# A hybrid layer step on one core: top-16 selection and norms cut into pieces and queued between weight splits, the output projection interleaved with the first query

## The chip, the cores and the metric

The kernel runs on one core of one Trainium2 chip. The metric is the device time of one execution in microseconds (us), the median of three runs. TensorE (PE) has two clock levels here, 1.2 and 2.4 GHz; the profile gives the granted clock as a share of the higher one.

## The reference, cut to what matters

One layer for two request groups that share all weights: 128 prompt tokens (one tile of 128) and 512 sample tokens (four tiles). After a mixer of a convolution and a recurrence, the layer projects with `w_out`, normalises, and runs a layer of product-key retrieved experts (PEER):

```python
y = jnp.concatenate([z, y_r], axis=-1) @ w_out
x = _layer_norm(ALPHA * x + g1 * y, ln1_g, ln1_b)
u = _layer_norm(x) * (1.0 + sc2) + sh2
...
q = (xb @ w_query).reshape(TOKEN_BLOCK, PEER_HEADS, 2, D_KEY)
s = jnp.einsum('chpd,hpnd->chpn', q, sub_keys).astype(jnp.float32)
sv, si = lax.top_k(s, PEER_TOPK)
cand = (sv[:, :, 0, :, None] + sv[:, :, 1, None, :]).reshape(TOKEN_BLOCK, PEER_HEADS, PEER_TOPK * PEER_TOPK)
top_s, top_pos = lax.top_k(cand, PEER_TOPK)
g = jax.nn.softmax(top_s, axis=-1).astype(xb.dtype)
act = jax.nn.gelu(jnp.einsum('chkd,cd->chk', jnp.take(peer_u, ids, axis=0), xb))
out = jnp.einsum('chk,chkd->cd', g * act, jnp.take(peer_v, ids, axis=0))
```

D is 2048, there are 8 heads with 2 x 128 sub-keys, 16384 experts, and 16 experts per head and token.

## The kernel before, in words

Every fp32 product is made of three fp32r products of high and low parts (`mm3`, L87 to L90), so each weight tile of 128x1024 is loaded by the SP queue (`load_w`, L80), split by ScalarE (ACT) into `whi` (L76) and by VectorE (DVE) into `wlo` (L77), and then used by 24 or 18 matmuls. There are three buffers for raw tiles and three for split ones. The tile framework writes each engine's instruction list ahead of time from the order of the program and a list scheduler; on the chip each engine goes through its list in order.

Tokens come in three parts. Tiles 0 and 1 are group B (`TB`, 256 columns), tiles 2 to 4 group A (`TA`, 384 columns). Of tile 1, 64 tokens are handled with the prompt tile by gathering their 128 expert rows from memory with indirect DMAs on the POOL queue (192 pairs of gathers of 1 MiB, `gather_gen`, L760; three row buffers, so DVE uses each in turn, L796 and L807). The other 448 tokens go through all experts densely: 256 weight halves for the scores (`s_half`, L865, called "S halves" here), 14 blocks of building the sparse gate matrix (L905 to L950, the G stage), and 256 steps with `peer_v` (the V stage, L1010 on).

The order of the stretch that the change touches, from the end of group B's output projection: `norm_pair` for tiles 0 and 1 (L698); `w_out` for group A, column groups 0 and 1 of four (L707, each column group has eight weight tiles of 18 matmuls); `query` for group B, heads 0 to 2 (L708); `w_out` column groups 2 and 3 (L709); `norm_a` for tiles 2 to 4 (L713); `query` for group B, heads 3 to 7 (L716); `query` for group A, all heads (L897), with eight S halves put in (`FILL`); then the G stage with the remaining S halves.

`query` (L602) takes, for each head and key half, two weight tiles, 48 matmuls into one bank, a copy to `qT`, a product with the sub-keys (L632), a copy to `s` (L634) and one `top16` per token tile, written right there; after both key halves it adds the candidates (L639), takes `top16` again, and finds indices and gates with one-hot products (L674, L676, L681). All of this is DVE work in the order of the program. `pace(rate)` (L852) advances the gathers by `rate` per weight half (0.5 in group A's query, 0.8 at S halves); what is left of them when the V stage begins is spread over its first 236 steps (`r_v`, L1008).

Of the kernel before, what the change touches and what calls it, by code (L numbers as in the profile page):

```python
# [34 lines left out]
def layer_kernel(ctx: ExitStack, tc: tile.TileContext, i: dict, y_p: bass.AP, y_s: bass.AP, st_o: bass.AP):  # L35
# [80 lines left out]
    def mm_bank():  # L116
        return ps_mm.tile([128, 512], F32, name="mm", tag="mm")
# [393 lines left out]
    def w_out(yh, yl, ts, ngs, rate=0.0):  # L511
        for ng in ngs:
# [6 lines left out]
            for kq in range(8):  # L519
                wh, wl = pre.pop(0) if pre else split(load_wo(kq, cs))  # L520
                for kk in range(2):
                    k = 2 * kq + kk
                    for n in range(len(ts)):
                        sl = slice(n * 128, (n + 1) * 128)
                        mk = mm3(banks[n], yh[:, k, sl], yl[:, k, sl], wh[:, kk, :], wl[:, kk, :], k == 0, k == KT - 1)
                if rate:
                    marks.append(mk)
                    pace(rate)
# [41 lines left out]

    def norm_a(hi, lo):
        sc, sh = modT[4], modT[3]
        for n, t in enumerate(TA):
            xx = x1[t]
            norm(cp, xx)
            for h in range(2):
                cs = slice(h * 1024, (h + 1) * 1024)
                V.tensor_tensor(xx[:, cs], xx[:, cs], ln1[0][:, cs], op=ALU.mult)
                V.tensor_tensor(xx[:, cs], xx[:, cs], ln1[1][:, cs], op=ALU.add)
            Q.dma_start(x1_d[t * 128:(t + 1) * 128, :], xx)  # L580
            norm(cp, xx)
            for q in range(4):
# [9 lines left out]
                V.tensor_tensor(lo[dst], u, hi[dst].bitcast(F32), op=ALU.subtract)  # L592

    def top16(vals, idx, src, n):
# [7 lines left out]
    def query(uh, ul, ts, heads, rate=0.0, fill=None):  # L602
        nt = len(ts)
        N = nt * 128
        o = OFF if ts[0] else 0
# [4 lines left out]
        for h in heads:  # L610
            kT = rt([2, 128], "kT")
            Q.dma_start(kT, i["keysT"][:, 2 * h:2 * h + 2, :])
            tv, ti = rt([3, 2, 16], "tv"), rt([3, 2, 16], "ti", U32)
            for p in range(2):
                m = 2 * h + p
                bank = mm_bank()
                for half in range(2):
# [10 lines left out]
                qT = rt([NA_TOK], "qT")  # L628
                S.copy(qT[:, 0:N], bank[:, 0:N])
                tp = tp_bank()  # L630
                for n in range(nt):
                    T.matmul(tp[:, n * 128:(n + 1) * 128], qT[:, n * 128:(n + 1) * 128], kT[:, p, :], start=True, stop=True)  # L632
                s = rt([NA_TOK], "s")
                S.copy(s[:, 0:N], tp[:, 0:N])  # L634
                for n in range(nt):
# [500 lines left out]
```

## Time and profile before

| what | us |
|---|---|
| median of 3 runs | 4084.11 (4066.59 to 4089.5) |
| the profiled execution | 4076.6 |
| its span from first to last instruction | 4074.5 |
| PE busy | 3806.5 (93%) |
| DVE busy | 3113.2 (76%) |
| ACT busy | 1590.9 (39%) |

The span is what the trace shows; the profiled execution's time has 2.1 us more around it. A busy PE is not PE at its peak, since matmuls are pipelined and run at either clock level. Busy shares are means over stages: the stretch that the change touches is from about 861 to 1500 us of the span.

### The profile page before, as it was taken

Reading aid. Unit: us, or ns where it says so; the run is one execution under the profiler, and the core shown is the slowest. Engines: PE = TensorE matmul, PEld = TensorE weight load, DVE = VectorE, ACT = ScalarE, POOL = GpSimd, SP = SyncE. Lnnn points to the kernel's source line nnn. Section 1 sums busy time; section 2 is a strip of 40 time slices with the busy share of each in tenths; the row PEclk is TensorE's granted clock in tenths of the full one; section 3 lists DMA queues with packets and bytes.
Section 4 is the critical chain, followed back from the end, with each engine's and each line's share of the span. In section 5 each row is a group of like instructions: output and inputs, shape, how many; then the busy total and the mean of one; then the engine's idle time right before and its main releaser. Section 6 shows DMA issues by size and latency. Waiting matters only on the chain.

```text
span 4074.5 us, 53954 instructions
## 1 busy us (share of the span) xinstructions
PE 3806.5 (93%) x20405; PEld 3380.9 (83%) x20405; DVE 3113.2 (76%) x4545; ACT 1590.9 (39%) x2701; POOL 689.2 (17%) x522
## 2 busy tenths in 40 slices
PE   7899899799868899999999999989999999999997
PEld 2688777678768789889998999878998899999896
DVE  4699964768699987777777777757787777877767
ACT  2111454433533365565655556533222222222222
POOL 0000111410001012222222222111211222221100
PEclk7899999899979899999999999999999999999998
DMA  9555444685435569888888988898888888888872
GB/s 365 203 200 178 140 163 153 191 262 200 150 117 206 195 235 312 291 312 309 306 311 280 323 316 310 307 320 293 311 324 315 285 314 310 311 310 315 312 216 88
DMA packets 408885, 1054.89 MB, mean 259 GB/s; under 512 B 27904, under 2 KB 253136, under 8 KB 355424
## 3 DMA queue, kind: packets, MB, share of 16 engines
q1 hardware_dynamic: 353328, 648.76, 47.2%
q0 software_dynamic: 55296, 402.68, 26.9%
q8 instruction: 160, 2.62, 0.3%
q14 instruction: 101, 0.83, 0.1%
HBM read 979.37 MB, written 71.38 MB: 258 GB/s over the span
## 4 chain that ended last, share of the span: by engine, by line
PE 56%; DMA 18%; DVE 14%; issue 7%; ACT 2%; POOL 2%; SPq 0%; POOLq 0%; DVEq 0%; ACTq 0%
PE vps L90 7%; PE vps L88 7%; PE vps L89 7%; PE sps L872 6%; PE sps L870 6%; PE sps L871 6%; DMA rows<-in_peer_v,ids 3%; DMA wa<-in_w_ada 3%; DVE wlo L77 3%; DMA wraw<-in_peer_uT 2%; DMA ge<-ge_d 2%; DMA rows<-in_peer_u,ids 2%; PE adab L156 2%; PE mm L90 2%; PE mm L89 2%
## 5 line engine op out<-in xcount | busy, mean ns | idle before, releaser
L76 ACT CAST whi<-wraw 128x1024 fp32r<-128x1024 f32 x704 | 737.1, 1049 | 1820.3 <-PE vps L89 475.4
L77 DVE TENSOR_TENSOR wlo<-wraw,whi 128x1024 fp32r<-128x1024 f32 x704 | 865.0, 1231 | 209.6 <-ACT whi L76 207.2
L870 PE MATMUL sps<-u2hi_a,whi 128*128 128x448 f32 x1984 | 732.5, 369 | 18.8 <-ACT whi L76 15.3
L872 PE MATMUL sps<-u2hi_a,wlo 128*128 128x448 f32 x1984 | 731.8, 369 | 5.8 <-DVE wlo L77 5.0
L871 PE MATMUL sps<-u2lo_a,whi 128*128 128x448 f32 x1984 | 730.7, 368 | 0.0
L807 DVE SCALAR_TENSOR_TENSOR gacc<-rows,coefs,gacc 128x2048 f32<-128x2048 f32 x190 | 446.3, 2349 | 197.9 <-DMA rows<-in_peer_v,ids 148.8
L796 DVE SCALAR_TENSOR_TENSOR rows<-rows,urow 128x2048 f32<-128x2048 f32 x192 | 439.3, 2288 | 172.2 <-DMA rows<-in_peer_u,ids 132.8
L870 PEld LDWEIGHTS sps<-u2hi_a,whi 128*128 128x128 f32 x1984 | 375.6, 189 | 52.8 <-ACT whi L76 17.1
L872 PEld LDWEIGHTS sps<-u2hi_a,wlo 128*128 128x128 f32 x1984 | 375.2, 189 | 44.3 <-DVE wlo L77 11.2
L88 PE MATMUL vps<-ehd,whi 128*128 128x448 f32 x1088 | 399.9, 368 | 12.0 <-ACT ehd L987 10.4
L90 PE MATMUL vps<-ehd,wlo 128*128 128x448 f32 x1088 | 400.4, 368 | 4.1 <-DVE wlo L77 4.1
L871 PEld LDWEIGHTS sps<-u2lo_a,whi 128*128 128x128 f32 x1984 | 375.8, 189 | 31.3
L89 PE MATMUL vps<-ehd,whi 128*128 128x448 f32 x1088 | 399.7, 367 | 0.0
L90 PE MATMUL vps<-ehl,wlo 128*128 128x448 f32 x960 | 353.8, 369 | 8.0 <-DVE wlo L77 8.0
L88 PE MATMUL vps<-ehl,whi 128*128 128x448 f32 x960 | 353.8, 369 | 6.3 <-ACT whi L76 4.8
L89 PE MATMUL vps<-ehl,whi 128*128 128x448 f32 x960 | 353.2, 368 | 0.0
L763 POOL DMA_INDIRECT rows<-in_peer_u,ids x128 | 186.8, 1460 | 962.6 <-PE sps L872 353.6
L942 ACT ACTIVATE A<-ab,gsp,nij 128x128 fp32r<-128x128 f32 x672 | 282.7, 487 | 1.2 <-DVE nij L922 1.1
L763 POOL DMA_INDIRECT rows<-in_peer_v,ids x128 | 182.4, 1425 | 542.9 <-PE sps L872 188.4
L88 PEld LDWEIGHTS vps<-ehd,whi 128*128 128x128 f32 x1088 | 204.8, 188 | 31.6 <-ACT ehd L987 10.8
L332 DVE SCALAR_TENSOR_TENSOR ybuf<-z,par,ybuf 128x655 f32<-128x655 f32 x240 | 220.6, 921 | 6.4
L90 PEld LDWEIGHTS vps<-ehd,wlo 128*128 128x128 f32 x1088 | 204.5, 188 | 24.7 <-DVE wlo L77 6.7
(301 smaller groups left out, 6719.2 us busy)
## 6 DMA issues: line engine op xcount, KB each, us to landing
wraw<-in_peer_uT SPq DMA_DIRECT2D x256, 512.0 KB, 6.4
wraw<-in_peer_v SPq DMA_DIRECT2D x256, 512.0 KB, 6.0
wa<-in_w_ada SPq DMA_DIRECT2D x192, 512.0 KB, 4.3
wraw<-in_w_in SPq DMA_DIRECT2D x64, 512.0 KB, 4.5
wraw<-in_w_out SPq DMA_DIRECT2D x64, 512.0 KB, 4.6
wraw<-in_w_query SPq DMA_DIRECT2D x64, 512.0 KB, 3.5
ge_d<-ge SPq DMA_DIRECT2D x128, 224.0 KB, 7.5
g_d<-gst SPq DMA_DIRECT2D x14, 2048.0 KB, 19.4
```

The source lines that it names most:

```text
L76: S.copy(hi, raw)
L77: V.tensor_tensor(lo, raw, hi.bitcast(F32), op=ALU.subtract)
L88: T.matmul(out, ah, bh, start=first, stop=False)
L89: T.matmul(out, ah, bl, start=False, stop=False)
L90: return T.matmul(out, al, bh, start=False, stop=last)
L763: d = G.indirect_dma_start(out=r, out_offset=None, in_=src, in_offset=bass.IndirectOffsetOnAxis(ap=idx, axis=0))
L796: V.scalar_tensor_tensor(r, r, 1.0, u, op0=ALU.mult, op1=ALU.mult, accum_out=dots[:, p:p + 1])
L807: V.scalar_tensor_tensor(acc, r, coef[:, p:p + 1], acc, op0=ALU.mult, op1=ALU.add)
L870: T.matmul(sps, wh[:, kk, :], u2hi_a[:, k, :], start=(k == 0), stop=False)
L871: T.matmul(sps, wh[:, kk, :], u2lo_a[:, k, :], start=False, stop=False)
L872: mk = T.matmul(sps, wl[:, kk, :], u2hi_a[:, k, :], start=False, stop=(k == KT - 1))
L942: S.activation(A[:, x], ab, AF.Relu, scale=nij[:, 1 + x, n:n + 1], bias=gsp[:, x, n:n + 1])
```

## The change

Three things change. First, `w_out` becomes a generator that yields after each weight tile. For group A, twelve of its 32 tiles run first, and the other twenty are put between the weight tiles of group B's query, whose eight heads now run in one go. Second, the top-16 work and `norm_a` become generators too: they are put in a list, `chores`, and each weight step calls `chore(us)`, which writes pieces of the first chores into the program until their stated costs have used up the credit. What is left after group A's query is written between S halves until the list is empty, and only then does the G stage begin; the count of S halves by then, `s_first`, replaces the constant 8. More buffers are given to scores and selections. Third, gathers start only once group B's chores are done (`b_done`), and are paced with 0.4 per weight half until all chores are done. The order of `norm_a` is changed too: first all three first norms, then all affines and second norms, then all transposes.

```diff
-    def w_out(yh, yl, ts, ngs, rate=0.0):
+    def w_out(yh, yl, ts, ngs):
...
-                if rate:
-                    marks.append(mk)
-                    pace(rate)
+                yield
...
+    chores, credit = [], [0.0]
+
+    def chore(us):
+        credit[0] += us
+        while chores and credit[0] > 0:
+            try:
+                credit[0] -= next(chores[0])
+            except StopIteration:
+                chores.pop(0)
+        if not chores:
+            credit[0] = min(credit[0], 0.0)
...
+    def tops(rp, tv, ti, s, p, nt):
+        for n in range(nt):
+            top16(rp, tv[:, n, p, :], ti[:, n, p, :], s[:, n * 128:(n + 1) * 128], 128)
+            yield 1.7
+
+    def choose(rp, h, tv, ti, ts):
...
+    def query(rp, uh, ul, ts, step, deep):
...
+            tv = rp.tile([128, nt, 2, 16], F32, name="tv", tag="tv", bufs=deep)
+            ti = rp.tile([128, nt, 2, 16], U32, name="ti", tag="ti", bufs=deep)
...
+                def scores(bank=bank, h=h, p=p, kT=kT, tv=tv, ti=ti):
+                    qT = rp.tile([128, N], F32, name="qT", tag="qT", bufs=2)
+                    S.copy(qT, bank[:, 0:N])
...
+                    s = rp.tile([128, N], F32, name="s", tag="s", bufs=2 * deep - 1)
+                    S.copy(s, tp[:, 0:N])
+                    chores.append(tops(rp, tv, ti, s, p, nt))
+                    if p:
+                        chores.append(choose(rp, h, tv, ti, ts))
...
-                    if rate:
-                        marks.append(mk)
-                        pace(rate)
-                    if fill:
-                        fill(m, half)
...
+                    marks.append(mk)
+                    while late:
+                        late.pop(0)()
+                    step(2 * m + half)
+                late.append(scores)
...
-    w_out(yhi_a, ylo_a, TA, (0, 1))
-    query(u2hi_b, u2lo_b, TB, range(3))
-    w_out(yhi_a, ylo_a, TA, (2, 3))
...
-    norm_a(u2hi_a, u2lo_a)
+    wo = w_out(yhi_a, ylo_a, TA, range(4))
+    for _ in range(12):
+        next(wo)
...
+    def step_b(n):
+        for _ in range(1 + (n % 4 == 3)):
+            if not u2_a and next(wo, 0) == 0:
+                u2_a.append(hla.tile([128, KT, ND], F32R, name="u2hi_a", tag="hla"))
+                u2_a.append(hla.tile([128, KT, ND], F32R, name="u2lo_a", tag="hla"))
+                chores.insert(0, norm_a(*u2_a))
+        chore(C_WO if not u2_a else C_NA)
+
+    C_WO, C_NA, C_QA, C_S = 3.6, 2.8, 2.6, 2.8
+    query(rpb, u2hi_b, u2lo_b, TB, step_b, 4)
+    while len(chores) and chores[0].__name__ == "norm_a":
+        chore(1.0)
...
-    query(u2hi_b, u2lo_b, TB, range(3, 8))
...
+    chores.append(b_end())
...
-    R_Q, R_A = 0.5, 0.8
+    R_Q, R_A = 0.4, 0.8
...
     def pace(n):
+        if not b_done[0]:
+            return
         due[0] += n
...
-                s_half(sps, e, half, R_A)
+                s_half(sps, e, half, rate[0])
...
-    FILL = (0, 1, 0, 0)
-    query(u2hi_a, u2lo_a, TA, range(8), R_Q, fill)
...
+    def step_a(n):
+        pace(R_Q)
+        chore(C_QA)
+
+    query(rpa, u2hi_a, u2lo_a, TA, step_a, 4)
+    while chores:
+        s_next()
+        chore(C_S)
+    rate[0] = R_A
+    s_first = nahead[0]
...
-                want = 8 + (8 * blk + t4 + 1) * (2 * NE - 8 - S_LATE) // (8 * NBLK_T)
+                want = s_first + (8 * blk + t4 + 1) * (2 * NE - s_first - S_LATE) // (8 * NBLK_T)
```

The stated costs, in us of credit: a `top16` of 128 scores 1.7, of candidates 1.6; the other pieces of `choose` 0.3 to 1.5 (10.2 in all for a head of group B, 13.2 for one of group A); `norm_a` 3.3 for a norm, 2.4 for half an affine, 0.7 for a group of four transposes, 42.6 in all.

## Rows read from the trace of the kernel before

**Rows 1.** The page: busy time of each engine over the span

```profile
PE 3806.5 (93%) x20405; PEld 3380.9 (83%) x20405; DVE 3113.2 (76%) x4545; ACT 1590.9 (39%) x2701; POOL 689.2 (17%) x522
```

**Rows 2.** Busy us by stretch (length, PE, PEld, DVE, ACT, POOL), clock, DMA, GB/s

```profile
860.80:943.90 83.10, 73.67 (x322) 59.40 (x321) 57.29 (x74) 29.03 (x28) 13.39 (x8) 0.96 0.81 273
943.90:982.60 38.70, 38.14 (x310) 37.09 (x309) 35.47 (x138) 18.88 (x34) 0.00 (x0) 1.00 0.53 176
982.60:1053.60 71.00, 67.94 (x294) 55.51 (x293) 45.15 (x116) 20.13 (x32) 0.00 (x0) 0.98 0.40 130
1053.60:1125.50 71.90, 56.87 (x386) 50.54 (x384) 55.11 (x81) 53.80 (x82) 6.67 (x6) 0.88 0.46 160
1125.50:1181.10 55.60, 28.00 (x183) 26.71 (x183) 53.73 (x291) 18.18 (x54) 0.00 (x0) 0.69 0.15 46
1181.10:1417.20 236.10, 202.50 (x1061) 192.77 (x1060) 227.29 (x811) 79.91 (x152) 26.61 (x24) 0.91 0.59 203
```

**Rows 3.** Waits between 944 and 1417 us: total, times, longest

```profile
PE mm L90 <- DVE wlo L77: 52.1, 11, 21.1
```

**Rows 4.** The same columns as Rows 2: the stretch of one wait

```profile
1147.40:1176.80 29.40, 2.58 (x13) 1.97 (x13) 29.40 (x172) 5.87 (x25) 0.00 (x0) 0.60 0.02 5
```

**Rows 5.** The same: PE undisturbed at w_out, group A's query, S halves

```profile
1000.00:1050.00 50.00, 50.00 (x223) 41.36 (x222) 25.43 (x42) 13.93 (x18) 0.00 (x0) 1.00 0.41 135
1347.50:1357.40 9.90, 9.90 (x58) 9.62 (x57) 9.87 (x33) 5.68 (x10) 1.58 (x1) 1.00 0.70 232
1420.00:1457.80 37.80, 37.80 (x187) 35.05 (x188) 35.50 (x83) 15.66 (x22) 8.10 (x5) 1.00 0.73 255
```

**Rows 6.** Timeline of DVE (start, us): last step of two heads of group B

```profile
1147.80 0.17 DVE L687 CAST ids<-r 128x32 uint32<-128x32 f32 x1
...
1159.95 0.17 DVE L687 CAST ids<-r 128x32 uint32<-128x32 f32 x1
```

**Rows 7.** Groups of DVE, 1181 to 1417 us (count, busy us, mean ns)

```profile
L77 DVE TENSOR_TENSOR wlo<-wraw,whi 128x1024 fp32r<-128x1024 f32 x38 | 46.0, 1211 | 1.5 <-ACT whi L76 1.4
L796 DVE SCALAR_TENSOR_TENSOR rows<-rows,urow 128x2048 f32<-128x2048 f32 x19 | 43.3, 2280 | 3.3 <-DMA rows<-in_peer_u,ids 3.3
```

**Rows 8.** Group B's low parts made by norm_pair: ns, first and last start

```profile
L569 DVE TENSOR_TENSOR u2lo_b<-tp,u2hi_b x8: 679/682/694, 892.4 to 936.1; 128x512 fp32r<-128x512 f32 x8
```

**Rows 9.** Group A's low parts made by norm_a: ns, first and last start

```profile
L592 DVE TENSOR_TENSOR u2lo_a<-ut,u2hi_a x12: 674/688/693, 1082.2 to 1127.2; 128x512 fp32r<-128x512 f32 x12
```

**Rows 10.** Groups of ACT, 1053 to 1128 us

```profile
L589 ACT ACTIVATE ut<-tp,modT,modT 128x128 f32<-128x128 f32 x48 | 19.9, 453 | 3.2 <-PE tp L588 1.9 <-DVE u2lo_a L592 0.3
L76 ACT CAST whi<-wraw 128x1024 fp32r<-128x1024 f32 x15 | 15.7, 1048 | 10.7 <-PE mm L89 7.3 <-DMA wraw<-in_w_query 3.3
L538 ACT ACTIVATE x<-x,nm,rstd 128x2048 f32<-128x2048 f32 x6 | 12.6, 2095 | 4.2 <-DVE nm L537 4.2
```

**Rows 11.** Groups of ACT: table loads of Exp (L651) and Gelu (L883)

```profile
L651 ACT ACT_TABLE_LOAD x6 | 7.7, 1283 | 0.1
L883 ACT ACT_TABLE_LOAD x6 | 7.7, 1283 | 0.1
```

**Rows 12.** The same columns: G stage; V stage while gathers run

```profile
1500.00:2740.00 1240.00, 1218.03 (x6080) 1115.59 (x6079) 924.64 (x950) 691.65 (x1407) 281.29 (x188) 0.99 0.88 306
2750.00:3880.00 1130.00, 1109.75 (x5378) 1014.06 (x5379) 885.34 (x932) 302.99 (x365) 223.93 (x163) 0.99 0.86 308
```

**Rows 13.** The page: the gathers' DMA queue, packets, MB, share of 16 engines

```profile
q0 software_dynamic: 55296, 402.68, 26.9%
```

**Rows 14.** The same columns: first, fastest, worst and last of 16 stretches

```profile
1800.00:1820.00 20.00, 20.00 (x102) 18.34 (x101) 15.16 (x17) 7.22 (x16) 4.93 (x3) 1.00 1.06 370
1980.00:2000.00 20.00, 20.00 (x103) 18.46 (x102) 13.35 (x17) 11.64 (x28) 5.23 (x4) 1.00 1.04 382
2160.00:2180.00 20.00, 14.88 (x71) 12.97 (x71) 9.48 (x10) 5.49 (x12) 3.11 (x2) 0.93 0.99 365
3840.00:3860.00 20.00, 20.00 (x100) 18.35 (x99) 13.79 (x14) 4.57 (x5) 2.88 (x3) 1.00 0.99 372
```

More of the change, by code (lines that the diff above doesn't have):

```diff
@@ L579, in norm_a @@
                 V.tensor_tensor(xx[:, cs], xx[:, cs], ln1[1][:, cs], op=ALU.add)
+                yield 2.4
             Q.dma_start(x1_d[t * 128:(t + 1) * 128, :], xx)
             norm(cp, xx)
+            yield 3.3
+        for n, t in enumerate(TA):
+            xx = x1[t]
             for q in range(4):
@@ L616, in query @@
                 bank = mm_bank()
+                def scores(bank=bank, h=h, p=p, kT=kT, tv=tv, ti=ti):
+                    qT = rp.tile([128, N], F32, name="qT", tag="qT", bufs=2)
+                    S.copy(qT, bank[:, 0:N])
+                    tp = tp_bank()
+                    for n in range(nt):
+                        T.matmul(tp[:, n * 128:(n + 1) * 128], qT[:, n * 128:(n + 1) * 128], kT[:, p, :], start=True, stop=True)
+                    s = rp.tile([128, N], F32, name="s", tag="s", bufs=2 * deep - 1)
[3 more added lines that the diff above has]
+                        chores.append(choose(rp, h, tv, ti, ts))
                 for half in range(2):
@@ L622, in query @@
                         mk = mm3(bank[:, 0:N], wh[:, kk, :], wl[:, kk, :], uh[:, k, o:o + N], ul[:, k, o:o + N], k == 0, k == KT - 1)
-                    if rate:
-                        marks.append(mk)
-                        pace(rate)
-                    if fill:
-                        fill(m, half)
[L628 to L632, printed above, removed]
@@ L683, in query @@
-            if ts[0] == 0:
-                for p in range(2):
-                    S.copy(ij[:, 0, p, hk], rs[p][:, 1, :])
-                V.scalar_tensor_tensor(rs[0], rs[0], 128.0, rs[1], op0=ALU.mult, op1=ALU.add)
-                V.tensor_copy(ids[:, :, hk], rs[0])
+                    marks.append(mk)
[3 more added lines that the diff above has]
+                late.append(scores)
+        while late:
+            late.pop(0)()
@@ L692, in layer_kernel @@
     for ng in range(4):
-        w_out(yhi_b, ylo_b, TB, (ng,))
+        for _ in w_out(yhi_b, ylo_b, TB, (ng,)):
+            pass
         if ng < 3:
@@ L700, in layer_kernel @@
     es_r = ExitStack()
-    rp = pool(es_r, "rp", 1, side="right")
+    rpb = pool(es_r, "rpb", 1, side="right")
     es_l = ExitStack()
@@ L721, in layer_kernel, with b_end @@
     es_hlb.close()
+    rpa = pool(es_r, "rpa", 1, side="right")
+    b_done = [False]
+    def b_end():
+        b_done[0] = True
+        yield 0.0
+    chores.append(b_end())
     gp = pool(ctx, "gp", 1)
@@ L874, in s_half @@
         pace(rate)
+    rate = [R_Q]
     def ahead_gen():
@@ L888, in layer_kernel, with s_next @@
     ag = ahead_gen()
-    def fill(m, half):
-        if FILL[2 * (m % 2) + half]:
-            next(ag, None)
-            nahead[0] += 1
     nahead = [0]
-    FILL = (0, 1, 0, 0)
-    query(u2hi_a, u2lo_a, TA, range(8), R_Q, fill)
+    def s_next():
+        next(ag, None)
+        nahead[0] += 1
+    def step_a(n):
[7 more added lines that the diff above has]
+    s_first = nahead[0]
     es_r.close()
```

135 lines of the change are left out of this document (71 added, 64 removed).

## The prediction

> **What bounds the kernel now.** The page comes first: PE is busy for 93% of the span and DVE for 76% [rows 1], so the time is PE's work plus its waits, and only waits can go. Then the busy time by stretch, from the end of group B's output projection (861 us) to the end of group A's query (1417 us), 556.4 us in six stretches [rows 2]. The reader is to see two columns against each other: where PE is far from full, DVE is full. In the last stretch DVE is busy for 227.3 of 236.1 us; in the one before, PE is busy for 28.0 of 55.6 us at a granted clock of 0.69. The list of waits names the pair: PE's matmuls waited 52.1 us for the DVE half of a weight split (`wlo`), 21.1 of it in one go [rows 3]. A stretch around that one wait shows why: DVE worked without a gap for 29.4 us, and PE for 2.6 [rows 4]. DVE was doing top-16 work of group B, one head each 12.15 us [rows 6], while the next split, 1.2 us long [rows 7], stood behind it in DVE's list. So the queries are bound by DVE in bursts, while the output projection beside them leaves DVE half idle (25.4 of 50 us, first of [rows 5]).
>
> How much PE loses there follows from its undisturbed pace. The output projection of group A is 4 x 8 x 18 = 576 matmuls at 50/223 = 0.224 us: 129 us. Group B's query ran three heads in the 38.7 us of the second of [rows 2], nearly undisturbed: 103 us for eight. Group A's query is 768 matmuls at 9.9/56 = 0.177 us (two of the 58 records only overlap an end): 136 us. Eight S halves of 24 matmuls at 37.8/185 = 0.204 us: 39 us. For group A's 96 key products and the 80 transposes I allow 20 us, 0.11 us each, below what three times their columns take [rows 5]. Sum 427 us, so 556 - 427 = **129 us** are waits and slow clock. This is the most that the change can win there.
>
> **The change part by part.** The count of instructions stays; places change. *First half of group B's query.* Sixteen of its 32 steps take the twenty remaining projection tiles. PE has 16 x 3.2 + 20 x 4.03 = 132 us. DVE has 36 splits (43 us), the projection's epilogues (18 operations of 512 columns, some 13 us, each taken as a little over half a split) and, by the credits, 57.6 us of stated cost; a head states 6.8 + 10.2 = 17.0 but takes 12.15 [rows 6], so this is 3.4 heads or 41 us. Sum 97 of 132: DVE no longer decides. Three projection banks must drain before the next column group finds three of five, and DVE's epilogue stands behind chores: I take 6 us for three changes.
>
> *Its start.* `norm_pair` delivers its last low part at 936.8 us [rows 8], 76 us after group B's projection; loads and POOL steps pace it and the change touches none of them. Before, sixteen projection tiles (64.5 us) and transposes covered this; now twelve do (48.4 us, with transposes 52). Query tiles then hold split buffers and wait; three buffers let about two more projection tiles pass (8 us). So PE waits about **16 us** (bounds 8 and 24), where it lost 14 before.
>
> *Second half.* `norm_a` now runs against sixteen steps of group B's query, 52 us of PE and 6 of transposes. Before, its last low part ended 74 us after the projection (1053.6 to 1127.9) [rows 2, 9]. ACT limits it: 19.9 + 12.6 us for `norm_a` without its casts, beside 16 splits (17 us) and the copies [rows 10], an estimated 60 us in all, of which the work behind the transposes comes last. Group A's query needs all of it. I take 74 - 58 = **16 us** of waiting (bounds 0 and 30). All `norm_a` work and its store on the SP queue go ahead of the chores in the list, so top-16 work of five heads is left over; its buffers (seven scores, four selections) hold it.
>
> *Group A's query.* By the credits its 32 steps of 2.6 us use up 83 us, about group B's leftover (20 top-16 passes and six selections, some 64 us of DVE). DVE then has 64 + 38 for splits in 146 us of PE. No gather runs here any more: `b_done` comes with the first S half. What is left, group A's eight heads, goes between **69 S halves** (I followed the credits step by step). A head of A takes about (227.3 - 46.0 - 43.3)/8 = 17 us [rows 2, 7]; DVE gets 138 + 69 x 1.2 + 28 gathers x 2.3 = 285 us against 69 x 4.9 = 338 of PE. I take 4 us of waits for both stretches together. If this cover fails and DVE stays the bound, it is the second rival.
>
> Exp and Gelu now alternate between the S halves. A table load takes 1.28 us, and the whole run has six of each here [rows 11]; sixteen at most would be 20 us on an ACT that needs per half 1.05 us for a split and half a Gelu, 1.3 of 4.9 us, so I take 0 (bounds 0 and 10). The Trainium skill speaks against it: "ScalarE: Activation LUTs", section "Table sets: the hidden batching unit", says to do all calls of one set before the next, at about 2.7 us a switch; by that an estimated 43 us of ACT time, and the sum would lose that if none were hidden. The trace shows 1.28 us with 0.1 us of idle time before, half of it.
>
> So of 129 us, 16 + 6 + 16 + 4 = 42 stay: **87 us won** up to the G stage.
>
> *G stage.* It has 177 S halves instead of 238 for the same 112 units. It now lasts 1240 us with 22 us lost; without 61 halves about 941, ACT at (692 - 79)/941 = 65% and DVE at (925 - 186)/941 = 79%, against 56% and 75% [rows 12]. Thinner cover, but nobody is full: **5 us** (bounds 0 and 15).
>
> *V stage.* Here the bill comes. `pace` had used 0.5 x 32 + 0.8 x 256 = 220 of 396 units by the V stage; now 0.4 x 69 + 0.8 x 187, about 176. So 220 units instead of 176 are spread over 236 steps: 0.93 per step, not 0.75. A gather takes 26.9% of 4074.5 us / 384 = 2.85 us of all sixteen transfer engines [rows 13]. A step lasts 1130 x 24/5378 = 5.04 us [rows 12], so the share rises by 0.186 x 2.85/5.04 = 0.105, from 0.86 to **0.965**, and the rate from 308 to 347 GB/s. What this costs, [rows 14] bound: from 1500 to 3880 us sixteen stretches of 20 us had a share of 0.97 or more (up to 382 GB/s), most with PE full, and PE lost 15.7 us in all of them, 4.9%, against 1.8% in the stages as a whole [rows 12]. If all 1189 us were like these, 3.1% or 37 us; if the mean does not matter, 0. I take the middle, **20 us**.
>
> The sum: 87 - 5 - 20 = **62 us faster**. The profiled execution would go from 4076.6 to about 4015; the median of the runs stands 7.5 us above it, and the forecast for the median is 4084 - 62 = **4022 us**.
>
> **The rivals.** *The V stage becomes bound by transfers.* This is the other side. Place: the 236 steps with gathers. It decides from where the engines sustain less than 347/(1 + 82/1189) = 325 GB/s, since 87 - 5 = 82 us is what it must eat. At no more than the present 308 GB/s the stage stretches by 12.7%, 151 us: 4153 us. For it: a mean share of 0.965 leaves nothing for bunching, and the worst stretch lost 5.1 of 20 us at 365 GB/s. Against: the first and the fastest of [rows 14] carried 370 and 382 GB/s with PE full. The Trainium skill, "DMA: Bandwidth & Descriptors", section "Where 436 GB/s comes from", puts the memory side at about 358 GB/s for a core; by that the V stage would just fit, and no row shows a hard stop there, since the fastest lies above it.
>
> *DVE stays the bound in group A's query*, because the scheduler writes ready top-16 pieces ahead of the splits whatever their place in the program. Then the last stretch keeps its loss, 236 - (136 + 10 + 39) = 51 us, and only 36 of the 87 are won: 36 - 5 - 20 = 11, **4073 us**. For it: DVE's list before already mixes two heads, so pieces do move. Against: those pieces stood ahead of the splits in the program too.
>
> *The order does not change at all* (the scheduler undoes the queue) and only the gathers move: 4084 + 20 = 4104 at worst, likelier within 0.5%. *No bill*: V stage and starts cost nothing, 4084 - 110 = 3974.
>
> **How the numbers follow.** My forecast (3985 to 4060) 0.68; no bill 0.07; DVE stays bound 0.13, of it 0.05 faster; transfers bound 0.08; order kept 0.04. A measurement of this kernel can tell about 0.5%, 20 us, from no change. Faster: 0.68 + 0.07 + 0.05 = 0.80; same: 0.08 + 0.04 = 0.12; slower 0.08. The range reaches down to the case without a bill and up over the DVE case, leaving the transfer rival out: 3970 to 4074.
>
> **What would show it.** Right: PE's waits for `wlo` before the G stage fall from 52 us to under 15; the G stage, which began after 17 S halves, starts some 170 us later (52 halves at 4.9 us less 87 us won); the V stage's DMA share is near 0.96 with 5.1 us a step. Wrong: a single PE wait above 20 us left in group B's query, DVE above 95% while PE waits in group A's query, or a V stage longer by over 60 us.

## The result and the profile after

The changed kernel takes 4001.07 us (median of 4 runs, 3993.8 to 4008.41) where the kernel before took 4078.56 beside it (4066.59 to 4089.5): a ratio of 0.983, 95% interval 0.9804 to 0.9856. That is 77.5 us faster; 62 were forecast, and 4001 lies inside the range. The profiled executions have spans of 3994.0 and 4074.5 us, 80.5 apart. The stages below are cut at the first and last matmul of each in the two traces:

| stretch | before | after | what changed in it | won |
|---|---|---|---|---|
| start to the end of group B's projection | 861.0 | 859.2 | nothing | 1.8 |
| to the end of group A's query | 554.0, with 8 S halves | 428.3, with none | chores spread, projection mixed in | 125.7 |
| to the first G tile | 50.8, with 8.9 S halves | 349.5, with 70.5 | group A's choices among S halves | -298.7 |
| to the start of V | 1284.3, with 239.1 S halves | 1013.3, with 185.4 | fewer S halves as cover | 271.0 |
| V stage | 1292.9 | 1312.3 | 220 units of gathers, not 176 | -19.4 |

First the page of the changed kernel, busy time of each engine and the DMA queues, against [rows 1, 13]:

```profile
PE 3775.8 (95%) x20405; PEld 3355.1 (84%) x20405; DVE 3104.1 (78%) x4545; ACT 1577.9 (40%) x2697; POOL 742.3 (19%) x522
...
q0 software_dynamic: 55296, 402.68, 27.2%
```

The count of PE and DVE instructions and the bytes gathered are the same: the work has only moved, and PE's share rises because the span shrinks. Next the stretches of the changed kernel that answer to [rows 2], with the same columns (length, busy PE, PEld, DVE, ACT, POOL, granted clock, DMA share, GB/s): the start of group B's query, the mix of query and projection, the second half of group B's query with `norm_a`, and group A's query.

```profile
858.60:945.70 87.10, 75.88 (x377) 62.53 (x376) 59.46 (x76) 31.22 (x31) 13.80 (x8) 1.00 0.83 275
945.70:1059.80 114.10, 113.80 (x676) 101.25 (x674) 92.55 (x279) 42.96 (x72) 0.00 (x0) 1.00 0.48 155
1059.80:1137.50 77.70, 67.39 (x453) 58.22 (x453) 74.20 (x225) 57.88 (x108) 6.69 (x6) 0.89 0.46 155
1137.50:1287.30 149.80, 143.92 (x848) 142.80 (x848) 148.95 (x638) 57.00 (x126) 0.00 (x0) 0.99 0.38 124
```

Read length minus PE busy down the rows: 11.2, 0.3, 10.3 and 5.9 us, where [rows 2] lost 9.4, 0.6, 3.1, 15.0, 27.6 and 33.6. The last row has DVE busy for 148.95 of 149.80 us, fuller than in the last of [rows 2], yet PE hardly waits: what DVE does there beside the splits can be late without PE noticing. PE's list of waits between 861 and 1290 us of the changed kernel (total, times, longest) says so:

```profile
PE tp L705 <- ACT qT L702: 7.8, 7, 2.7
PE tp L604 <- ACT ut L605: 5.5, 12, 1.1
...
PE mm L89 <- DVE wlo L77: 1.9, 3, 1.0
PE mm L90 <- DVE wlo L77: 1.8, 1, 1.8
```

[rows 3] has L90 alone; with the 3.1 us of L89 and the 1.0 of L872 PE waited 56.2 us for `wlo` before, 21.1 of it in one go. Now it is 3.7, none longer than 1.8. Most of the waiting before lay in group A's query. Cut at that query's first and last matmul, the stretch before and after, and PE's waits in it before:

```profile
1148.20:1415.00 266.80, 207.74 (x1082) 197.42 (x1080) 257.99 (x990) 84.53 (x176) 25.67 (x23) 0.87 0.53 182
...
1131.80:1287.50 155.70, 149.82 (x870) 147.95 (x871) 153.91 (x654) 61.21 (x139) 0.00 (x0) 0.97 0.36 119
...
PE mm L90 <- DVE wlo L77: 42.5, 8, 21.1
```

Less the eight S halves (39.2 us) this query fell from 227.6 to 155.7 us, 71.9 of the 86.5 won up to its end. DVE was nearly full in it before and after, but it has 104 us less to do there now: the gathers' operations (47 us) and the splits of the eight S halves are gone from it, and much of group A's choices waits for the S halves behind it. Then the stretches of group A's choices, of the start of the G stage, of all of it, and of the V stage while gathers run, which answer to [rows 12]:

```profile
1287.30:1387.30 100.00, 99.16 (x489) 90.64 (x488) 99.28 (x348) 40.89 (x71) 8.08 (x7) 1.00 0.58 196
1387.30:1632.60 245.30, 243.93 (x1205) 225.28 (x1203) 106.40 (x89) 65.01 (x78) 26.51 (x22) 1.00 0.65 223
...
1637.00:1671.00 34.00, 33.55 (x170) 30.50 (x171) 25.79 (x32) 29.47 (x69) 7.67 (x5) 1.00 0.69 244
1637.00:2640.00 1003.00, 976.54 (x4907) 896.00 (x4907) 787.58 (x869) 652.67 (x1402) 220.57 (x149) 0.99 0.87 305
...
2650.30:3800.00 1149.70, 1115.79 (x5389) 1014.70 (x5390) 972.79 (x994) 303.16 (x365) 340.22 (x206) 0.99 0.95 341
```

Two things are to be seen. DVE's chores are over by about 1387 us, although the program spreads them over S halves that run to 1632: the scheduler pulls them forward into whatever room DVE has. And the V stage, at a DMA share of 0.95 and 341 GB/s, lost 33.9 of 1149.7 us of PE (2.9%) where [rows 12] lost 20.3 of 1130 (1.8%). The last stretch ahead of the G stage in the kernel before, and the stage's start, not among the rows ahead of the prediction, belong beside the second and the third line:

```profile
1415.00:1465.80 50.80, 44.68 (x223) 40.84 (x223) 48.40 (x106) 20.70 (x32) 10.14 (x7) 1.00 0.77 271
1465.80:1500.00 34.20, 28.28 (x117) 23.94 (x118) 30.08 (x40) 31.29 (x78) 6.04 (x3) 0.77 0.49 170
```

At the start of the stage PE ran 117 matmuls in 34.2 us at a mean clock of 0.77 (between its two levels of 1.2 and 2.4 GHz), after waits; now it runs 170 in 34.0 at full clock.

### The profile page after: what moved, and what is told of

Read it like the earlier page. It is cut to its first block, busy times and chain, and to the rows that moved or that the text cites. A ratio compares the mean times of both kernels' runs of the same rounds, so it can differ in the third digit from the quotient of the medians.

```text
span 3994.0 us, 53950 instructions
## 1 busy us (share of the span) xinstructions
PE 3775.8 (95%) x20405; PEld 3355.1 (84%) x20405; DVE 3104.1 (78%) x4545; ACT 1577.9 (40%) x2697; POOL 742.3 (19%) x522
## 4 chain that ended last, share of the span: by engine, by line
PE 53%; DMA 20%; DVE 15%; issue 7%; ACT 2%; POOL 1%; SPq 0%; DVEq 0%; POOLq 0%; ACTq 0%
PE sps L931 5%; PE sps L929 5%; PE sps L930 5%; PE vps L90 5%; PE vps L88 5%; PE vps L89 5%; DVE wlo L77 4%; DMA wa<-in_w_ada 4%; DMA ge<-ge_d 3%; DMA gt<-g_d 2%; DMA rows<-in_peer_v,ids 2%; DMA wraw<-in_peer_uT 2%; PE mm L931 2%; PE mm L930 2%; PE mm L929 2%
## 5 line engine op out<-in xcount | busy, mean ns | idle before, releaser
L929 PE MATMUL sps<-u2hi_a,whi 128*128 128x448 f32 x1488 | 548.9, 369 | 14.4 <-ACT whi L76 12.5
L931 PE MATMUL sps<-u2hi_a,wlo 128*128 128x448 f32 x1488 | 549.4, 369 | 7.9 <-DVE wlo L77 7.8
L930 PE MATMUL sps<-u2lo_a,whi 128*128 128x448 f32 x1488 | 547.6, 368 | 0.0
L90 PE MATMUL vps<-ehd,wlo 128*128 128x448 f32 x1088 | 401.8, 369 | 6.8 <-DVE wlo L77 6.8
L89 PE MATMUL vps<-ehd,whi 128*128 128x448 f32 x1088 | 401.0, 369 | 0.0
L90 PE MATMUL vps<-ehl,wlo 128*128 128x448 f32 x960 | 354.2, 369 | 20.8 <-DVE wlo L77 20.8
L89 PE MATMUL vps<-ehl,whi 128*128 128x448 f32 x960 | 351.9, 367 | 0.0
L929 PEld LDWEIGHTS sps<-u2hi_a,whi 128*128 128x128 f32 x1488 | 282.3, 190 | 38.0 <-ACT whi L76 13.7
L931 PEld LDWEIGHTS sps<-u2hi_a,wlo 128*128 128x128 f32 x1488 | 281.8, 189 | 37.4 <-DVE wlo L77 13.7
L930 PEld LDWEIGHTS sps<-u2lo_a,whi 128*128 128x128 f32 x1488 | 282.1, 190 | 22.2
L820 POOL DMA_INDIRECT rows<-in_peer_v,ids x128 | 197.3, 1541 | 533.9 <-PE gps L1014 162.9
L90 PEld LDWEIGHTS vps<-ehd,wlo 128*128 128x128 f32 x1088 | 205.4, 189 | 28.9 <-DVE wlo L77 10.9
```

Source lines behind the costliest of these rows:

```text
L89: T.matmul(out, ah, bl, start=False, stop=False)
L90: return T.matmul(out, al, bh, start=False, stop=last)
L820: d = G.indirect_dma_start(out=r, out_offset=None, in_=src, in_offset=bass.IndirectOffsetOnAxis(ap=idx, axis=0))
L929: T.matmul(sps, wh[:, kk, :], u2hi_a[:, k, :], start=(k == 0), stop=False)
L930: T.matmul(sps, wh[:, kk, :], u2lo_a[:, k, :], start=False, stop=False)
L931: mk = T.matmul(sps, wl[:, kk, :], u2hi_a[:, k, :], start=False, stop=(k == KT - 1))
```

## The experiments

All times are medians, each with its ratio to the kernel before on the same chip, where that took between 4063 and 4079 us; so kernels that ran on different chips compare by their ratios (the change has 0.983, 0.9804 to 0.9856). Lengths of stages are those of the one profiled execution of a kernel; the V stage's runs from the first to the last `vps` matmul.

**1. Fewer gathers left for V.**

```diff
-    rate = [R_Q]
+    rate = [R_A]
```

> The changed kernel with one number different: gathers at the S halves that carry the leftover chores are paced at 0.8 per half, not 0.4, so that 191 units instead of 220 are left for the V stage (0.81 per step, not 0.93). Theory (the V stage grew by 19.5 us because its transfer engines are at a mean share of 0.95): the V stage shrinks from 1311 to about 1298 us, the S halves with chores stay at 345 us although their DMA share rises from 0.63 to about 0.86, and the time falls by about 13 us, to 3988. Rival (the V stage grew for another reason, such as DVE at 83% of it): V stage 1306 to 1315 us, time 3996 to 4006.

Measured: 3965.02 us, ratio 0.9759 (0.9732 to 0.9786), V stage 1286.3 us. The V stage is back at about the length of before, 12 us below what was expected. The time is below that of the changed kernel by some 29 us by the ratios, where 13 were expected. That is for the theory, but runs 8, 11 and 12 limit how much this one point may carry.

**2. No mix.**

```diff
-    for _ in range(12):
+    for _ in range(32):
```

> The changed kernel with all 32 tiles of group A's output projection ahead of group B's query instead of twelve, so that nothing of it is mixed with the query; the queue of chores stays. Theory (the queue is what wins; DVE's work only has to go somewhere with room, and the S halves after the queries have room): about as fast, 3975 to 4010, with shorter waits at the start of group B's query and for the second norms, and DVE a little over PE in group B's query. Rival (the mixing is what wins, because it is the projection that gives DVE its room): 64 us of DVE time are lost beside the projection and come back as PE waits in the queries, 4030 to 4065.

Measured: 3996.02 us, 0.9847 (0.9811 to 0.9883). From the end of group B's projection to the end of group A's query it took 418.8 us, 9.5 less than the change, and then 356.5 to the G stage, 7.0 more. With the mix undone, the gain is the same: mixing the projection with the query isn't what wins.

**3. No queue.** All chores run where they are made; the mix, the larger buffers and the pieces stay.

```diff
-    C_WO, C_NA, C_QA, C_S = 3.6, 2.8, 2.6, 2.8
+    C_WO, C_NA, C_QA, C_S = 1e6, 1e6, 1e6, 1e6
```

> The changed kernel with the four credits set so high that every chore is written into the program at once where it arises, as before the change; mixing, buffers and the late key products stay. No S half is then ahead of the G stage, and gathers run in group A's query at 0.4. Theory (the queue wins): group A's query is bound by DVE again, 8 heads at some 25 us against 18 us of PE, and the norms stand ahead of the splits in one block; 4055 to 4085. Rival (mixing and deeper buffers win): 3995 to 4020.

Measured: 4044.64 us, 0.9953 (0.993 to 0.9976), between the two expectations, though nearer the theory's. What was waited for is back. PE's longest item between 863 and 1368 us of this kernel, and its second query stretch in the columns of [rows 2]:

```profile
PE mm L90 <- DVE wlo L77: 50.0, 11, 11.6
```

```profile
1164.20:1366.20 202.00, 163.04 (x864) 159.63 (x863) 200.58 (x809) 60.81 (x137) 15.04 (x12) 0.87 0.47 158
```

DVE is full here too (200.58 of 202.00), as it is in the changed kernel; but PE is now idle for 39.0 us and its clock falls to 0.87. The two kernels differ by the place of the chores and by what hangs on it (here twelve gathers run in that stretch, some 26 us of DVE). DVE has 46.8 us more to do in this query than in the changed kernel's, and the query is 46.4 us longer. So here it is DVE's total that decides, and the queue wins by letting that work fall due later. From the end of group B's projection to the end of group A's query it took 500.9 us against 428.3: the queue is worth 73 us there, of which the fuller V stage (1292.6 us here, 1312.3 with the queue) takes 20 back and the S halves with the G stage 10 (1352.5 us here, 1362.8 with it). That leaves 43; the ratios to the kernel before put it at some 50 (0.9953 against 0.983).

**4. The kernel before, without gathers in its query.**

```diff
-    R_Q, R_A = 0.5, 0.8
+    R_Q, R_A = 0.0, 0.8
```

> The kernel before with one number different: no gathers in group A's query (pace 0 instead of 0.5); they move to the V stage (0.81 per step, not 0.75). DVE is relieved of 19 operations of 2.3 us, 43 us, in the 236 us of that query. Theory (DVE's total decides there): group A's query shrinks by 30 to 40 us, the V stage grows by some 7 us, the time falls to about 4050. Rival (the order of DVE's list decides, not its total: each burst of top-16 work still stands ahead of the splits): the query shrinks by less than 15 us and the time stays within 4065 to 4085.

Measured: 4039.0 us, 0.9946 (0.9924 to 0.9968). The wait list of PE, 861 to 1390 us, keeps the big item; the line below it is group A's query, in the columns of [rows 2]:

```profile
PE mm L90 <- DVE wlo L77: 42.6, 8, 21.1
...
1153.60:1391.90 238.30, 197.58 (x1082) 188.30 (x1080) 232.39 (x954) 84.05 (x175) 9.59 (x8) 0.91 0.42 142
```

Sixteen units of gathers less take 28 us off the stretch (526.2 against 554.0) but only 9.5 of the 52.1 us of waits for `wlo`, and the one of 21.1 us not at all. The rival (less than 15 us, 4065 to 4085) fails; the theory comes out near its numbers (30 to 40 us, about 4050). In group A's query DVE was busy for 232.4 us instead of 258.0, 25.6 less, and the query took 28.5 us less (238.3 against 266.8): about one for one, as in run 3. So DVE's total decides there. What the order of its list does by itself no run shows: none kept the same work in the query and changed only its order. The V stage, with 16 more gathers in the trace (178 against 162), was no longer for them: 1291.1 us against 1292.9.

**5. The kernel before, with the V stage's gathers of the change.**

```diff
-    R_Q, R_A = 0.5, 0.8
+    R_Q, R_A = 0.5, 0.625
```

> The kernel before with one number changed: the S halves pay 0.625 gather units each instead of 0.8, so that by the program's count 220 units instead of 176 are left for the V stage, as in the changed kernel, and everything else stays in its place. Theory (the fuller transfer engines of the V stage cost time by themselves): V stage 1310 to 1318 us instead of 1293, its DMA share about 0.95, and the whole 10 to 20 us slower than the kernel before (about 4075 to 4085 where before is 4063), since the G stage gains little from fewer gathers. Rival (the V stage of the changed kernel is longer for another reason, such as what the queue left late): V stage unchanged within 5 us, the whole unchanged or a little faster. Second rival (the G stage wins back what V loses): V longer by 20, and 1417 to 2750 shorter by 15 or more.

Measured: 4053.55 us, 0.9978 (0.9963 to 0.9992). Its G and V stages, columns as before:

```profile
1457.00:2707.90 1250.90, 1233.91 (x6189) 1132.90 (x6189) 863.72 (x929) 726.66 (x1487) 191.76 (x150) 0.99 0.80 276
2707.90:3860.00 1152.10, 1118.49 (x5390) 1017.54 (x5391) 975.27 (x997) 303.67 (x365) 340.27 (x206) 0.99 0.94 341
```

The V stage took 1312.6 us instead of 1292.9: 19.7 us of bill, with nothing moved but gathers, at the share (0.94) and rate (341 GB/s) of the changed kernel. The G stage took 1250.8 instead of 1284.3, 33.5 less, for 42 gathers fewer (0.175 x 239). The second rival holds: a gather costs in the G stage too, 0.80 us against 0.45 (19.7/44) in V. This run also shows the grain of a single profile: its stretch from group B's projection to the end of group A's query has the same work as the kernel before and took 542.5 us, not 554.0. The 86.5 us that the queries won by the table (125.7 less 39.2 for eight S halves) could thus be 75.

**6. More gathers beside all S halves.**

```diff
-    R_Q, R_A = 0.4, 0.8
+    R_Q, R_A = 0.4, 1.0
...
-    rate = [R_Q]
+    rate = [1.0]
```

> The changed kernel with 1.0 gather units per S half throughout (0.4, then 0.8, in the change; 0.8 throughout in the first experiment), so that 140 of 396 units are left for the V stage, 0.59 a step. Theory (gathers are free as long as the transfer engines have room, and cost only above a share of about 0.9): the V stage has no more to win below 0.81 a step, 1280 to 1290 us, while the halves of the S work, 4.9 us each with 2.9 us of gather beside their own loads, now have a share near 0.9 or above and lose 0 to 15 us; time 3960 to 3985, no better than the 3965 of 0.8. Rival (every gather taken from V pays, since PE waits there for loads): V falls by another 15 us or more, time 3945 to 3955. Second rival (gathers beside the queue of chores delay DVE or POOL): the stretch from group A's query to the G stage is longer by 15 us.

Measured: 4041.02 us, 0.994 (0.992 to 0.9959). The stretch of the choices, the G stage and the V stage:

```profile
1288.70:1644.00 355.30, 347.05 (x1704) 317.47 (x1702) 300.06 (x508) 113.09 (x158) 103.35 (x70) 1.00 0.93 335
1644.00:2740.10 1096.10, 1001.12 (x4907) 913.93 (x4907) 872.62 (x928) 655.36 (x1407) 316.80 (x185) 0.95 0.90 317
2740.10:3880.00 1139.90, 1137.99 (x5566) 1046.31 (x5567) 847.28 (x913) 312.26 (x373) 177.13 (x131) 1.00 0.82 283
```

V is shorter than expected (1264.0 us) with PE full, which is for the rival; but the G stage is 81 us longer than in run 1 (1096.1 against 1015.1) for 37 gathers, 2.2 us each. Run 1's G stage, for comparison:

```profile
1646.70:2661.80 1015.10, 977.61 (x4908) 899.17 (x4908) 793.76 (x873) 654.20 (x1404) 228.05 (x148) 0.98 0.88 304
```

All theories missed that: the 15 us expected at most for the S work hold for the stretch ahead of G alone, which took 355.3 us against 352.1, at a share of 0.93.

**7. Runs 1 and 2 in one** (`range(32)` and `rate = [R_A]`).

> The first two experiments in one: all 32 steps of the output projection ahead of group B's query, and 0.8 gather units per S half throughout. If the two are independent the time is that of 0.8 alone, 3965, less what the unmixed order gave (5 us, which could not be told from nothing): 3955 to 3970. If the mix does protect something (the chores then all run in group A's query, with 4.9 us halves and gathers behind them), 3970 to 3985.

Measured: 3980.26 us, 0.9788 (0.9762 to 0.9814), V stage 1298.6 us. The median lies in the second expectation, by which the mix protects something; but its interval overlaps that of run 1, so whether the mix is worth anything isn't settled. By the medians it would be some 15 us.

**8. Run 1 with denser chores.**

```diff
-    C_WO, C_NA, C_QA, C_S = 3.6, 2.8, 2.6, 2.8
+    C_WO, C_NA, C_QA, C_S = 3.6, 2.8, 2.6, 5.6
```

> The changed kernel with 0.8 units per S half throughout and 5.6 us of chores instead of 2.8 after each S half: about 35 S halves instead of 70 then stand ahead of the G stage, the other 35 go between its tiles, and DVE's list of chores is denser. The trace of the changed kernel shows DVE with all chores done by about 1385 us although the S halves run on to 1632, so the spacing in the program is no longer what spaces them. Theory (the scheduler packs the chores as DVE finds room; the S halves behind them have cover to spare): the stretch up to the G stage loses nothing (idle below 12 us), the G stage keeps more cover and wins 0 to 10 us: 3955 to 3968, against 3965 with 2.8. Rival (the spacing is what protects the splits): PE waits for wlo in that stretch grow by 20 us or more, time 3980 or above.

Measured: 4015.46 us, 0.9888 (0.9863 to 0.9913), 50 us above run 1. The rival's time is met, but not its mechanism. From the end of group A's query to the V stage it took 1371.9 us against 1367.2, and in the stretch of the choices PE was idle for 4.0 us; the V stage took 1308.4 against 1286.3, with the same number of gathers by the program. The profiles (spans 4002.7 and 3979.5) thus show 23 of the 50 us, 22 of them in a stage that the edit doesn't touch. They show so little because run 1's profiled execution is its slowest (3981.32, where its other four took 3964 to 3967) and run 8's its fastest (4004.45 of up to 4030.29): a stage of one profile stands for the median only to within some 15 us.

**9. Gathers where they seemed cheapest.**

```diff
-    R_Q, R_A = 0.4, 0.8
+    R_Q, R_A = 0.4, 0.65
...
-    rate = [R_Q]
+    rate = [1.0]
```

> The changed kernel with the gathers put where the runs so far found them cheapest: 1.0 unit per S half ahead of the G stage (there 0.8 and 1.0 cost the same 352 and 355 us), 0.65 in the G stage (in the kernel before, 42 fewer gathers there made it 33 us shorter), which leaves about 206 of 396 for the V stage, 0.87 a step. Theory (a gather costs only where the transfer engines are nearly full, and the G stage is the dearest place): the G stage falls from 1015 to 985 to 1000 us, the V stage is 1295 to 1308, the time 3945 to 3965. Rival (the sum of the transfers is what counts, and moving gathers between the stages wins nothing more): G as much shorter as V is longer, 3965 to 3985.

Measured: 3969.69 us, 0.9753 (0.973 to 0.9777). The same three stretches:

```profile
1290.00:1640.00 350.00, 345.69 (x1686) 315.25 (x1686) 295.12 (x477) 113.05 (x157) 96.52 (x68) 1.00 0.92 332
1640.00:2635.00 995.00, 977.46 (x4950) 901.74 (x4949) 739.37 (x840) 658.75 (x1406) 167.15 (x123) 0.99 0.82 285
2635.00:3780.00 1145.00, 1107.15 (x5365) 1007.68 (x5364) 941.64 (x968) 301.41 (x358) 332.48 (x194) 1.00 0.92 331
```

The G stage fell to 983.1 us, as expected, but V rose to 1316.2; together 2299.3 against 2301.4 of run 1. The rival holds: the time is no better than run 1's, and the two stages together are the same within what single profiles tell. The first and the third line have the same share, 0.92; PE lost 1.2% in one and 3.3% in the other. A share by itself doesn't price a gather; the stage does.

**10. Half of DVE's work on the gathered rows in V, all transfers kept.**

```diff
+    cw = [D]
...
-            V.scalar_tensor_tensor(r, r, 1.0, u, op0=ALU.mult, op1=ALU.mult, accum_out=dots[:, p:p + 1])
+            w = cw[0]
+            V.scalar_tensor_tensor(r[:, 0:w], r[:, 0:w], 1.0, u[:, 0:w], op0=ALU.mult, op1=ALU.mult, accum_out=dots[:, p:p + 1])
...
-                V.scalar_tensor_tensor(acc, r, coef[:, p:p + 1], acc, op0=ALU.mult, op1=ALU.add)
+                w = cw[0]
+                V.scalar_tensor_tensor(acc[:, 0:w], r[:, 0:w], coef[:, p:p + 1], acc[:, 0:w], op0=ALU.mult, op1=ALU.add)
...
+        cw[0] = D // 2
         r_v = left[0] / (NE // 4 * 8 - 2 * sizes[-1] - 4)
```

> The changed kernel, with the two DVE operations on a gathered row working on 1024 of its 2048 columns in the V stage (the output for those tokens leaves out the other half of the sums); the gathers and all their transfers stay. It tells what the V stage's 20 us are: the transfers, or DVE's share (973 of 1150 us busy in the changed kernel against 885 of 1130 before). Theory (transfers): DVE's busy time in the V stage falls by about 170 us, the V stage stays at 1305 to 1318 us and the time at 3995 to 4010. Rival (DVE): the V stage falls to 1285 to 1295, the time to 3975 to 3985.

Measured: 4006.55 us, 0.985 (0.9824 to 0.9876). Its V stage:

```profile
2665.00:3815.00 1150.00, 1106.82 (x5344) 1007.50 (x5344) 758.74 (x988) 298.64 (x362) 242.34 (x204) 0.99 0.94 339
```

DVE is busy for 758.74 us where the changed kernel had 972.79, and the V stage is no shorter (1321.8 us, 4 above the theory's range). The bill isn't DVE's, and the time lies in the theory's range. Up to the V stage this kernel is the changed one, and yet its profiled execution took 11.6 us more for that part (2661.9 against 2650.3): so far apart can two executions be. The waits of ACT for the next weight tile in a V stretch, first of before (2780 to 4000 us), then of the change (2680 to 3900), and PE's wait for the split behind it in each, say through whom:

```profile
ACT whi L76 <- PE vps L89: 449.6, 137, 7.9
...
ACT whi L76 <- DMA wraw<-in_peer_v: 125.2, 35, 9.2
...
PE vps L90 <- DVE wlo L77: 12.2, 12, 3.1
```

```profile
ACT whi L76 <- DMA wraw<-in_peer_v: 374.9, 100, 14.1
ACT whi L76 <- PE vps L89: 192.0, 66, 5.7
...
PE vps L90 <- DVE wlo L77: 27.6, 31, 3.0
```

Before, the split mostly waited for PE to free its buffer, so loads were early. Now it mostly waits for the load, in 100 of some 240 steps, and where the buffers don't absorb it PE waits for `wlo`, 27.6 us against 12.2. PE's item names DVE in both kernels; the transfer stands two steps behind it, ahead of ACT's half of the split.

**11. The changed kernel with denser chores** (5.6 for the last credit, gather rates as in the change).

> The changed kernel with 5.6 us of chores after each S half instead of 2.8 and its own gather rates (0.4, then 0.8): some 35 S halves ahead of the G stage instead of 70, and by the program's count about 206 units left for the V stage instead of 220. With 0.8 throughout, the same edit cost 50 us by the medians (4015 against 3965), but the profiles showed only 23 of it, 22 in the V stage, whose gathers the edit does not touch. Theory (denser chores cost time themselves, in a way that a single profile does not show): 4030 to 4055, against 4001 of the changed kernel. Rival (the edit is neutral but for where gathers fall, and the 50 us belong to that one pair of kernels): 3990 to 4010.

Measured: 3999.23 us, 0.9846 (0.9811 to 0.9881). Neutral: the rival holds, and density alone doesn't cost the 50 us of run 8.

**12. Run 1 with sparser chores** (1.9 for the last credit).

> The changed kernel with 0.8 units per S half throughout and 1.9 us of chores after each S half instead of 2.8: about 103 S halves ahead of the G stage instead of 70, so that 153 instead of 186 are left to cover the G tiles. If denser chores cost time, sparser ones win or are the same: 3950 to 3970, against 3965. Rival (the G tiles need the cover: in the G stage ACT and DVE are needed for G's own 112 units beside the splits): the G stage loses 10 to 25 us more, 3975 to 3995.

Measured: 4004.76 us, 0.9851 (0.9821 to 0.988), worse than both expectations. To the start of V it took 1390.2 us after group A's query, 23.0 more than run 1, 10 of them as more idle time in the G stage (47.9 us against 37.5), as the rival said; the V stage took 1295.7, 9.4 more.

Runs 1, 7, 8 and 12 all pay 0.8 units throughout and stand at 3965, 3980, 4015 and 4005; the change and runs 2 and 11 pay 0.4 first and stand at 4001, 3996 and 3999. The V stage is shorter in the first set (1286 to 1308 us against 1312 to 1324), but in the whole time only runs 1 and 7 keep it. Nor does it go by the count of gathers alone: run 11 has 192 in V by its trace, 14 fewer than the change, and the longest V of these. Which small shift of loads against gathers makes the 50 us between runs 1 and 8 wasn't found and stays open. Runs 1 and 9 are versions that beat both kernels (3965 and 3970 us); a rule behind them beyond "not 1.0 in the G stage" isn't shown.

## Why the prediction was right, point by point

**The diagnosis** (PE waits for splits that stand behind other DVE work) held, but bursts are only half of it. The waits for `wlo` of [rows 3] went from 52.1 to 3.7 us, under the 15 that were asked for; run 3 brought them back by giving up the queue alone, and run 2 showed that the mix could go. But 42.5 of the 52.1 us lay in group A's query. Of these, 21.1 stood behind one burst of group B's work; over the whole query DVE was busy for 258.0 of 266.8 us, and its total was too much. Before and in runs 4 and 3, that query lasts little longer than DVE's work in it (266.8 for 258.0, 238.3 for 232.4, 202.1 for 200.7 us). In the change it is 155.7 for 153.9, but there PE is busy for 149.8 us and limits too. The other signs came as well: the G stage starts 171 us later (1637.0 against 1465.8), where some 170 were said. One sign of being wrong was half met, since DVE was above 95% in group A's query, but PE's waits for `wlo` were gone.

**The queries, 87 won:** 86.5 by the table, 554.0 less 39.2 for eight S halves, 514.8, against 428.3 now. The four terms compare as follows. Start 16: idle 11.2. Bank changes in the mix 6: 0.3; three waits were costed that hardly occurred. `norm_a` 16: 10.3 idle at a clock of 0.89, which costs some more. Group A's query and the S halves with chores 4: 5.9 and 3.5. Measured idle in the queries is 27.7 us where waits and slow clock were to be 42 in all, and 40.5 were lost (428.3 against the 387.8 of undisturbed work); the rest lies in the slow clock and in the 20 us allowed for transposes and key products, and wasn't taken apart. With the terms this far off, a sum that is right to half a microsecond is luck.

**Group A's query** failed in its reasoning and not in its result. The prediction had DVE at 102 of 146 us there, by the credits. It was at 148.95 of 149.80, because the scheduler wrote later pieces forward; PE waited for no split longer than 1.8 us, so they did not stand in the splits' way. The rival that named this mechanism took it to be harmful: in the trace it wasn't.

**The G stage, 5 lost:** this is the step that failed, by its size and sign. From the end of group A's query to V the change took 27.7 us more (1362.8 against 1335.1), for 8 more S halves; with 39.2 us for these, 11.5 were won. The cover term itself was right: 36.7 us of idle time are left in 1013.3 us where 38.0 were in 1284.3, so at the old share (3.0%) 30 would be left, and the thinner cover cost about 7. What was missing is the start of the stage. In the kernel before it ran at a clock of 0.77 with 117 matmuls in 34.2 us; now it runs 170 in 34.0, and the 53 more, at the 0.204 us of [rows 5], are 11 us. Some 6 more were idle time just ahead of it, in the 50.8 us that began at 1415.0. That start could have been read ahead of the change: the [rows 12] for the G stage begin at 1500, just behind it. Why it now starts without a gap (DVE's leftover choices stood ahead of it before, and none do now) is argued from the trace and wasn't tried by itself.

**The V stage, 20 lost:** 19.4, at a share of 0.95 and 1149.7 x 24/5389 = 5.12 us a step, as the prediction asked. Run 5 charged it alone (19.7) and run 10 excluded DVE. The size was a middle between two bounds, equal gathers gave V stages up to 22 us apart in runs 1, 7, 8 and 12, and the first 16 gathers more cost nothing in run 4, so its exactness is luck; that there is such a bill is not.

**The transfer rival** (V at 308 GB/s, 4153 us) needed a limit below 325 GB/s; V carried 341, at a price of 1.5% of the stage. The Trainium skill, "DMA: Bandwidth & Descriptors", section "Where 436 GB/s comes from", has about 358 GB/s as the memory's limit for a core. V lies below it, but the changed kernel carries 381 GB/s from 10 to 110 us of its span, at a share of 0.99, so no run here shows that figure as a limit. **The case without a bill** had 110 us, which don't follow from its terms: 87 and the 16 of the start, less 5, are 98, and 114 if `norm_a`'s 16 are a start too. **The table loads**, allowed up to 10 us, didn't grow: in the changed kernel Exp and Gelu load four times each, where [rows 11] had six, again 1283 ns with 0.1 us before:

```profile
L645 ACT ACT_TABLE_LOAD x4 | 5.1, 1283 | 0.1
L944 ACT ACT_TABLE_LOAD x4 | 5.1, 1283 | 0.1
```

The Trainium skill's rule against mixing sets ("ScalarE: Activation LUTs", "Table sets: the hidden batching unit") had little to act on: the choices, packed into 100 us by the scheduler, brought fewer alternations than there were before.

So of the 18.5 us by which the profiles beat the sum of 62, 16.5 are the G stage (5 lost against 11.5 won), 0.6 V, and 1.8 lie ahead of everything that was changed, while the queries fall 0.5 short.

## What to carry to other kernels

Where PE waits in one stage for small operations of a nearly full engine, look at what else stands in that engine's in-order list and when it falls due. Work that isn't needed in that stage can be cut into pieces and queued so that it runs behind the splits and ends in a stage with room; that wins the waits without removing an instruction, and an engine that then shows 99% need not be the bound, because the rest of its work can wait. What is pushed out of one stage arrives in another: follow every counter that is shared across stages (here the gathers) and price it where it lands, by that stage's own load. And before a variant's 1% is believed, change something else beside it: here an edit that was neutral in one kernel (run 11) came with 50 us in another (run 8).

## What was not expected of the hardware

The price of a gather depends on the stage more than on the share of the transfer engines: next to nothing ahead of the G stage up to a share of 0.93 (70 S halves in 349.5, 352.1 and 355.3 us with about 28, 56 and 70 gathers), 0.8 to 1.15 us each in the G stage between some 0.65 and 0.8 units per half (run 5; runs 9 and 1 with 983.1 and 1015.1 us, 28 gathers) and 2.2 us between 0.8 and 1.0. In that last case the share was only 0.90. Equal gathers gave G stages from 1008 to 1022 us (the change, runs 1, 2, 7 and 10), so the smaller prices are rough. What the G stage has and the stretch ahead of it hasn't, among others the writing of its results, wasn't separated.

And run 10: with DVE's operations on the gathered rows cut to 1024 columns, one of them went from 2285 to 1222 ns, and the time taken from DVE turned into idle time ahead of its next loads. The two kernels' DVE groups in their V stages (2680 to 3900 us; count, busy us, mean ns, idle time before), first of the change and then of run 10:

```profile
L853 DVE SCALAR_TENSOR_TENSOR rows<-rows,urow 128x2048 f32<-128x2048 f32 x94 | 214.8, 2285 | 29.8 <-DMA rows<-in_peer_u,id 16.9 <-DMA rows<-in_peer_u,ids 9.2 <-DMA urow<-u_d 3.7
...
L1053 DVE TENSOR_TENSOR ge<-ge,gt 128x448 f32<-128x448 f32 x118 | 70.0, 620 | 97.5 <-DMA ge<-ge_d 51.4 <-DMA gt<-g_d 45.8
```

```profile
L1057 DVE TENSOR_TENSOR ge<-ge,gt 128x448 f32<-128x448 f32 x120 | 72.1, 622 | 227.2 <-DMA gt<-g_d 165.4 <-DMA ge<-ge_d 61.7
...
L856 DVE SCALAR_TENSOR_TENSOR rows<-rows,urow 128x1024 f32<-128x1024 f32 x94 | 114.9, 1222 | 69.4 <-DMA rows<-in_peer_u,id 54.6 <-DMA rows<-in_peer_u,ids 14.7
```

DVE's idle time ahead of `ge` rose from 97.5 to 227.2 us, nearly all of it on loads, and nothing ended sooner for it: a DVE with less to do won nothing in this stage.
